# One layer of a hybrid decoder on one core: another order of the two plain feature groups, tile norms on VectorE, the keys' short product in another bank, and the last tiles worked in halves

## The chip, the cores and the metric

The kernel runs on one core of a Trainium2 chip. Time is device time of one execution, in microseconds (us); smaller is better. Six names of queues and engines return throughout: PE (TensorE, the matrix multiplications and transposes), PEld (its weight loads), DVE (VectorE), ACT (ScalarE), POOL (GpSimd) and SP (SyncE, which here only issues transfers). Each engine works through its own instructions in a fixed order and waits, at the head of that order, for what its next instruction needs.

## The reference

One layer is computed for 1024 prompt tokens with 16 meta tokens ahead of them, and for 64 sample tokens: 1104 tokens of width 1024, all in fp32.

```python
def rms_norm(x, g):  # cut
    return x * rsqrt(mean(x * x, -1) + eps) * g
def half_ffn(h, g_pre, g_post, w_gate, w_up, w_down):
    return h + 0.5 * rms_norm(swiglu(rms_norm(h, g_pre), w_gate, w_up, w_down), g_post)
# run_layer
h = half_ffn(h, ffn1_...)
y, st = token_mixer(rms_norm(h, mix_norm_pre), ...)   # u @ w_in, gated DeltaNet, sliding-window attention, @ w_out
h = h + rms_norm(y, mix_norm_post)
h = half_ffn(h, ffn2_...)
```

The hidden width of either FFN is 2816. In the DeltaNet branch each head's keys are convolved, normalised and multiplied with themselves (`kk = k k^T`, per chunk), decayed and solved against.

## The kernel before

**Precision and tiles.** Every large product is made of fp32r operands that are split into a high and a low part (`xh`, `xl`, `wh`, `wl`), with three matmuls for one. ACT rounds to the high part, DVE or POOL subtracts to get the low part. Tokens come in nine tiles of 128 rows, the last of them short, and go into the FFNs as two halves of tokens.

**Gate and up.** The 22 groups of 128 hidden features are worked in 11 pairs, `f` = 0 to 10. One pair takes, for gate and for up, seven block products instead of eight (Strassen's scheme in Winograd's form): the products `p` = 1 to 7 land in the PSUM banks A, B and C, and DVE adds them into `u2g`, `sg`, `u3g` and the like (`gate_up`, L322). `hidden(f)` (L364) then makes gate times up (on POOL, `times`) and writes to DRAM the operands that the down product reads: seven of them, with the sums `S1` and `S2`, for most pairs, but only four and no sums for the two pairs in `plain`, which are 9 and 10. Each operand is a tile `hs` (four buffers), made of a high part and a DVE subtraction, and stored to `hid`. The work of `hidden(f)` is issued step by step among the products of the pair after it. The first two pairs start while the tokens are still being transposed (`start`, L446): of these `up` (L458) then makes only the products 6, 5, 7, 4 and 3.

**Down.** `down` (L500) loads `hb` tiles from `hid` on SP's queue and `raw` weights on the same queue, and adds the products into `acc`. Pairs 9 and 10 are the last group, with plain products.

**Tails.** After the first FFN each tile of tokens is transposed back (L582), normed, added to the residual (`post_norm`, L618), normed again for the mixer (`pre_norm`, L94) and transposed again (L105). A norm is a square-and-sum on ACT (L81), two tiny POOL operations (L82, L83) for the factor, and a multiplication. In `pre_norm` the multiplication by the gain is POOL's (L99), that by the factor ACT's (L101). After the second FFN, tiles 0 to 5 are finished among the last down products, and tiles 6, 8 and 7 behind them; only tile 7 is normed in halves (`last_norm`, L625).

**Mixer.** `before` (L809) projects the beta/decay columns and the first two heads' keys while the tails run. `w_in` (L766) loads a weight column, rounds it on ACT (L773) and subtracts on POOL (L774). `gates` (L819) turns beta and decays into factors. For each head `keys` (L962) transposes the convolved keys into PSUM tiles tagged `tr`, and multiplies keys by keys into tiles `pk` (two buffers): two of 128-row blocks (L1008), and one 80x80 product of the 80 tokens that are left over (L1014). DVE reads each `pk` (L1010, L1015). `decays` (L951) adds masks on POOL (L954). Then a triangular solve runs lane by lane on DVE (`lane_solve`, L1058) beside the sliding-window attention (`swa_kv` L1104, `swa_block` L1201).

**What sets the order.** PE's order is the program's own: generators are merged by `weave` with written shares. On the other engines a scheduler of the compiler orders the instructions, except where the code pins one (`keep_in_program_order`) or holds it behind another (`issue_after`).

**The start.** The gain of the first norm comes as one row of 4 KB on ACT's queue, and PE spreads it over 128 partitions by two matmuls (L1907); DVE copies it to SBUF (L1908).

## Time and profile before

| | |
|---|---|
| median of 3 runs | 2791.03 us (2784.93 to 2792.57) |
| the profiled execution | 2782.66 us, its span 2780.8 us |
| mean granted TensorE clock | 0.982 |
| PE busy | 2663.7 us (96% of the span) |
| DVE, ACT, POOL busy | 1586.3, 1096.9, 1389.3 us |

The span runs from the first to the last instruction that the profiler saw; 1.9 us of the execution lie outside it. The profiled execution is 0.3% faster than the median of the three runs. A gap of an engine is the idle time just before an instruction, put down to what ended it last. Times of places below are us from the start of the span.

### The profile page before, as it was taken

What the parts mean: (1) busy time and instruction counts of PE and PEld (TensorE: products, weight loads), DVE (VectorE), ACT (ScalarE), POOL (GpSimd) and SP (SyncE); (2) the same over time, 40 slices, a digit from 0 to 9 for tenths busy, and PEclk for the clock granted to TensorE, in tenths of its full rate; (3) what the DMA queues carried; (4) which work ended last, traced back from release to release, by engine and by line L of the source; (5) the groups of instructions that cost most, each with busy time, mean ns of one, the idle gap of its engine ahead of it and who ended that gap; (6) DMA issues with size and microseconds to landing.
All of it is one profiled execution on the core that took longest, in us unless ns stands there. A gap on an engine that the chain in (4) does not pass through costs nothing. (4 is left out here: it accounts for less than half of the span.)

```text
span 2780.8 us, 49379 instructions
## 1 busy us (share of the span) xinstructions
PE 2663.7 (96%) x18961; PEld 2495.5 (90%) x18961; DVE 1586.3 (57%) x2381; ACT 1096.9 (39%) x2584; POOL 1389.3 (50%) x1297
## 2 busy tenths in 40 slices
PE   7999999999978998999999999998999999999998
PEld 6999999999977887788788888887789999999998
DVE  6666565345556759964544444443557566553566
ACT  5343343322154642354444444444443343334221
POOL 5555555445455744654434434435455555554472
PEclk9999999999988999999999999999999999999999
DMA  4343343577533652354323333334443343427763
GB/s 139 134 156 134 141 161 120 200 232 241 180 130 114 200 186 92 101 175 116 107 84 93 90 96 95 92 90 133 138 138 137 138 159 132 145 112 296 241 232 139
DMA packets 229412, 405.96 MB, mean 146 GB/s; under 512 B 59719, under 2 KB 121319, under 8 KB 228888
## 3 DMA queue, kind: packets, MB, share of 16 engines
q1 hardware_dynamic: 208870, 324.23, 36.0%
q10 hardware_dynamic: 20306, 78.57, 7.1%
q8 instruction: 150, 2.46, 0.4%
q14 instruction: 86, 0.70, 0.1%
HBM read 263.84 MB, written 140.53 MB: 145 GB/s over the span
## 5 line engine op out<-in xcount | busy, mean ns | idle before, releaser
L281 POOL TENSOR_TENSOR wl<-T,wh 128x512 fp32r<-128x512 f32 x246 | 330.5, 1349 | 345.1 <-ACT wh L280 254.4
L133 PE MATMUL gu<-xh,wl 128*128 128x512 f32 (+3 forms) x1456 | 500.5, 344 | 0.1
L129 PE MATMUL gu<-xh,wh 128*128 128x512 f32 (+3 forms) x1456 | 496.6, 341 | 0.0
L131 PE MATMUL gu<-xl,wh 128*128 128x512 f32 (+3 forms) x1456 | 496.0, 341 | 0.0
L495 PE MATMUL y<-hb,wh 128*128 128x256 f32 (+2 forms) x2528 | 432.2, 291 | 8.5 <-DMA hb<-hid 7.3
L281 POOL TENSOR_TENSOR wl<-raw,wh 128x512 fp32r<-128x512 f32 x200 | 281.5, 1414 | 248.8 <-ACT wh L280 198.8
L495 PEld LDWEIGHTS y<-hb,wh 128*128 128x128 f32 x2528 | 367.6, 189 | 10.4 <-DMA hb<-hid 7.9
L133 PEld LDWEIGHTS gu<-xh,wl 128*128 128x128 f32 x1456 | 280.7, 193 | 28.4 <-issue 11.1
L280 ACT CAST wh<-T 128x512 fp32r<-128x512 f32 x246 | 152.4, 620 | 377.5 <-PE B L315 117.0
L131 PEld LDWEIGHTS gu<-xl,wh 128*128 128x128 f32 x1456 | 280.5, 193 | 19.6 <-issue 1.2
L129 PEld LDWEIGHTS gu<-xh,wh 128*128 128x128 f32 x1456 | 280.5, 193 | 18.4 <-issue 1.6
L495 PE MATMUL y<-hb,wl 128*128 128x256 f32 (+2 forms) x1264 | 272.4, 289 | 0.0
L280 ACT CAST wh<-raw 128x512 fp32r<-128x512 f32 x200 | 122.2, 620 | 286.4 <-PE C L315 87.8
L506 DVE TENSOR_TENSOR acc<-acc,y 128x552 f32<-128x552 f32 (+4 forms) x216 | 145.1, 679 | 149.2 <-PE y L495 148.7
L774 POOL TENSOR_TENSOR wl<-raw,wh 128x1024 fp32r<-128x1024 f32 x60 | 144.7, 2412 | 145.5 <-ACT wh L773 126.1
L495 PEld LDWEIGHTS y<-hb,wl 128*128 128x128 f32 x1264 | 208.0, 189 | 0.0
L255 DVE TENSOR_TENSOR T<-raw,raw 128x512 f32<-128x512 f32 x124 | 120.9, 979 | 120.8 <-POOL wl L281 120.3
L1536 POOL TENSOR_TENSOR f<-f,mhalf 128x1 f32<-128x1 f32 (+1 forms) x72 | 54.4, 756 | 112.0 <-DVE f L1534 106.5
L266 DVE TENSOR_TENSOR T<-raw,T 128x512 f32<-128x512 f32 x62 | 64.4, 1042 | 59.5 <-POOL wl L281 59.5
L927 DVE SCALAR_TENSOR_TENSOR cv<-pc,cw,cv 128x1131 f32<-128x1131 f32 x48 | 75.2, 1568 | 34.2 <-POOL cv L924 33.8
L255 DVE TENSOR_TENSOR T<-raw,T 128x512 f32<-128x512 f32 x62 | 66.7, 1082 | 32.6 <-POOL wl L281 32.4
L1067 DVE TENSOR_TENSOR la<-la,ltmp 72x14 f32<-72x14 f32 (+37 forms) x76 | 80.1, 1054 | 1.3
(589 smaller groups left out, 7408.5 us busy)
## 6 DMA issues: line engine op xcount, KB each, us to landing
hb<-hid SPq DMA_DIRECT2D x71, 552.0 KB
hb<-hid SPq DMA_DIRECT2D x71, 544.0 KB
hid<-hs ACTq DMA_DIRECT2D x69, 552.0 KB
hid<-hs ACTq DMA_DIRECT2D x69, 544.0 KB
raw<-in_w_in_dram SPq DMA_DIRECT2D x58, 512.0 KB
raw<-in_ffn_w_gate_dram SPq DMA_DIRECT2D x100, 256.0 KB
raw<-in_ffn_w_up_dram SPq DMA_DIRECT2D x94, 256.0 KB
raw<-in_ffn_w_down_dram SPq DMA_DIRECT2D x88, 256.0 KB
```

Source lines behind the costliest of these rows:

```text
L129: nc.tensor.matmul(ps, wh, xh, start=first and i == 0, stop=False)
L131: nc.tensor.matmul(ps, wh, xl, start=False, stop=False)
L133: nc.tensor.matmul(ps, wl, xh, start=False, stop=last and i == n - 1)
L255: self.nc.vector.tensor_tensor(out=b[name], in0=b[x], in1=b[y], op=ALU.subtract)
L266: nc.vector.tensor_tensor(out=s, in0=b["21"], in1=s, op=ALU.subtract)
L280: self.nc.scalar.copy(hi, s)
L281: self.nc.gpsimd.tensor_tensor(out=lo, in0=s, in1=f32(hi), op=ALU.subtract)
L495: self.nc.tensor.matmul(self.view(ps[d], (i,)), w[x][:, d * P:(d + 1) * P], hb[:, y, lo:hi], start=j + x + y == 0, stop=j == len(items) - ...
L506: dve = lambda out, x, y: nc.vector.tensor_tensor(out=out, in0=x, in1=y, op=ALU.add)
L774: nc.gpsimd.tensor_tensor(out=lo, in0=raw, in1=f32(hi), op=ALU.subtract)
L927: nc.vector.scalar_tensor_tensor(out=cv, in0=pc[:, w:w + PADW], scalar=self.cw[:, j, w:w + 1], in1=cv, op0=ALU.mult, op1=ALU.add)
L1067: nc.vector.tensor_tensor(out=a[:n, 0:j, j + 1:size], in0=a[:n, 0:j, j + 1:size], in1=t, op=ALU.add)
```

## The change

Nine things are edited.

1. The pairs of either FFN are worked in the order 9, 0, 1, ..., 8, 10 (`self.order`): one plain pair first, the other last. For the last pair, gate times up is on DVE for two of the three products. A hold on the second pair's steps (`issue_after(self.sixth)`) is taken out.
2. The gain of the first norm is loaded as a broadcast of 512 KB on SP's queue, behind the first two tiles and ahead of the first weights. The row, the two matmuls and the two copies go.
3. In `sixth_ahead` the three loads are pinned; in `down` the weight difference `T1` of the first group is pinned.
4. `pre_norm` multiplies by gain and factor in one DVE instruction (L100 of the changed kernel) instead of one on POOL and one on ACT.
5. The rounding and subtraction of head 1's weights (column 9) is held behind the norm of the tile that comes before.
6. `gates` yields once more and is woven in three steps from 0.5 on instead of two from 0.75; the exponential of `ea` is pinned.
7. The keys' 80x80 product goes into the `tr` tile of the last transposes, which has three buffers now; `pk` serves the 128-row blocks alone. The masks of head 1 and later are pinned.
8. The third group of transposes of the sliding window's keys and values goes into a tile `po` instead of `pt`.
9. After the second FFN, tiles 0 to 3, and 4 and 5, are finished earlier; tiles 6, 8 and 7 are finished in halves of 512 features, the first halves among the last down products, and the second halves of 6 and 8 use PSUM tiles of the down products (`y`).

```diff
+        self.order = (plain[0], *(f for f in range(NF // 2) if f not in plain), plain[1])
...
-    nc.gpsimd.tensor_tensor(out=out[:n], in0=x[:n], in1=g[:n], op=ALU.mult)
     r = rstd(c, pool, x, n, 1.0 / D, EPS, "n")
-    nc.scalar.activation(out[:n], out[:n], AF.Copy, scale=r[:n, 0:1])
+    nc.vector.scalar_tensor_tensor(out=out[:n], in0=x[:n], scalar=r[:n, 0:1], in1=g[:n], op0=ALU.mult, op1=ALU.mult)
...
             if len(parts) == 2 and p != 6:
-
-                with self.c.tc.issue_after(self.sixth) if p in (7, 4) and (f, kind) == self.begun else nullcontext():
-                    next(self.late, None)
+                next(self.late, None)
...
         def times(key):
-            nc.gpsimd.tensor_tensor(out=g[key], in0=g[key], in1=u[key], op=ALU.mult)
+            (nc.vector if f == self.order[-1] and key != "u3" else nc.gpsimd).tensor_tensor(out=g[key], in0=g[key], in1=u[key], op=ALU.mult)
...
-                        self.difference(x, "T1", "12", "11")
+                        self.difference(x, "T1", "12", "11", c.tc.keep_in_program_order if vi == 0 else lambda op: op)
...
-        self.ready = {8 + h: self.w_in(8 + h, self.nc.scalar) for h in range(2)}
+        raw = [self.w_load(8 + h, self.nc.scalar) for h in range(2)]
+        self.ready = {8: self.w_in(8, raw[0])}
+        tc = self.c.tc
+        with tc.issue_after(self.c.last_square), tc.issue_after(self.c.last_factor):
+            self.ready[9] = self.w_in(9, raw[1])
...
                 nc.tensor.transpose(pt[:80, 0, :], k8, self.k(C_IDENT))
+                nc.tensor.matmul(pt[:80, 1, 0:80], k8, k8, start=True, stop=True)
...
-                nc.tensor.matmul(pk[:80, 0, 0:80], k8, k8, start=True, stop=True)
-                nc.vector.scalar_tensor_tensor(out=b8, in0=pk[:80, 0, 0:80], scalar=ns[:80, 8:9], in1=dt[:80, 8, 0:80],
+                nc.vector.scalar_tensor_tensor(out=b8, in0=pt[:80, 1, 0:80], scalar=ns[:80, 8:9], in1=dt[:80, 8, 0:80],
...
-                before = [(gates, 0.75, 1, 2)]
+                before = [(gates, 0.5, 1, 3)]
...
-                    pt = self.ps([P, 4, P], "pt", 2)
+                    pt = self.ps([P, 4, P], "pt", 2) if t0 < 8 else self.ps([P, 4, P], "po")
...
-                if t == 0:
-                    row, one = c.t(xin, [1, D], tag="row", bufs=1), c.t(xin, [1, P], tag="one", bufs=1)
-                    nc.scalar.dma_start(row, I["ffn1_norm_pre"])
...
+                if t == 1:
+                    gain("ffn1_norm_pre", xin)
...
+        def last_tiles(pool):
+
+            g, state = gain("ffn2_norm_post", pool), {}
+            for h, t in ((h, t) for h in range(2) for t in (6, 8, 7)):
+                n, cols = f2.rows[t], slice(512 * h, 512 * h + 512)
+                if (h, t) in ((1, 6), (1, 8)):
+                    ps = c.t(f2.psy[0], [P, 1024], tag="y").rearrange("p (k t) -> p k t", t=P)[:, 0:4]
+                else:
+                    ps = c.t(ptr, [P, KD, P], tag="tr")[:, 0:4]
+                f2.feature_half(ps, t, h)
...
+                nc.scalar.activation(dump[:n, cols], src[:n], AF.Square, accum_out=r2[:n, h:h + 1])
+                nc.vector.tensor_tensor(out=y[:n, cols], in0=src[:n], in1=g[:n, cols], op=ALU.mult)
...
-        weave((dn, 0, 1, 15), (f2.tail_steps(ptr, nrm, finish2, (0, 1, 2, None, 3, None, 4, 5)), 0.05, 0.95, 8))
-        drain(f2.tail_steps(ptr, nrm, finish2, (6, 8, 7)))
+        last = last_tiles(nrm)
+        weave((dn, 0, 1, 15), (f2.tail_steps(ptr, nrm, finish2, (0, 1, 2, 3)), 0, 0.46, 4),
+              (f2.tail_steps(ptr, nrm, finish2, (4, 5)), 0.5, 0.7, 2), (steps_of(last, 3), 0.68, 1, 3))
+        drain(last)
```

What this does to the order of instructions is shown at three places. A row is the source line, the operation, and out<-in with buffer numbers; lines behind the edits are numbered a few lower or higher in the changed kernel.

The first place is DVE in the first FFN, up to the sum `u3g` of the second pair's gate, which PE's bank C waits for. `S`, `hs` and the product with `g_` belong to `hidden` of the first pair. Before:

```order
L266 TENSOR_TENSOR T_1340<-raw_1336,T_1340 128x512
L353 TENSOR_TENSOR u2g_1184<-sg_561,B_1159 128x552
L372 TENSOR_TENSOR hs_1255<-S_198_1137,hs_1255 128x552
L372 TENSOR_TENSOR sg_241<-g_80_312,sg_241 128x552
L255 TENSOR_TENSOR T_1559<-raw_1517,raw_1515 128x512
L372 TENSOR_TENSOR hs_1292<-sg_241,hs_1292 128x552
L353 TENSOR_TENSOR sg_561<-u2g_1184,B_1226 128x552
L372 TENSOR_TENSOR hs_1326<-S_197_1136,hs_1326 128x552
L372 TENSOR_TENSOR hs_1437<-g_134_678,hs_1437 128x552
L358 TENSOR_TENSOR u3g_1252<-sg_561,C_1190 128x552
```

The same place in the changed kernel:

```order
L369 TENSOR_TENSOR hs_1127<-sg_232,hs_1127 128x552
L369 TENSOR_TENSOR hs_1203<-u2g_818,hs_1203 128x552
L369 TENSOR_TENSOR hs_1410<-g_130_669,hs_1410 128x552
L267 TENSOR_TENSOR T_1314<-raw_1310,T_1314 128x512
L354 TENSOR_TENSOR u2g_1171<-sg_552,B_1146 128x552
L256 TENSOR_TENSOR T_1532<-raw_1490,raw_1488 128x512
L354 TENSOR_TENSOR sg_552<-u2g_1171,B_1212 128x552
L357 TENSOR_TENSOR u3g_1238<-sg_552,C_1177 128x552
```

Between `u2g` and `u3g` stand two instructions now, where seven stood; the sums `S` of the first pair are gone.

The second place is POOL among the tails of the first FFN. `rp` is the factor of `post_norm`, `rn` that of `pre_norm`, `wl` the low part of a `w_in` weight column. Before:

```order
L774 TENSOR_TENSOR wl_8974<-raw_8971,wh_8973 128x1024
L774 TENSOR_TENSOR wl_8980<-raw_8977,wh_8979 128x1024
L82 TENSOR_SCALAR rp_8892<-rp_8892 128x1
L83 TENSOR_TENSOR rp_8892<-rp_8892,mhalf_64 128x1
L99 TENSOR_TENSOR res_8890<-acc_863_5982,g_mix_norm_pre_8245 128x1024
L82 TENSOR_SCALAR rn_8901<-rn_8901 128x1
L82 TENSOR_SCALAR rp_9042<-rp_9042 128x1
L83 TENSOR_TENSOR rn_8901<-rn_8901,mhalf_64 128x1
L83 TENSOR_TENSOR rp_9042<-rp_9042,mhalf_64 128x1
L99 TENSOR_TENSOR acc_864_5983<-y_9041,g_mix_norm_pre_8245 128x1024
```

In the changed kernel:

```order
L764 TENSOR_TENSOR wl_8963<-raw_8958,wh_8962 128x1024
L82 TENSOR_SCALAR rp_8880<-rp_8880 128x1
L83 TENSOR_TENSOR rp_8880<-rp_8880,mhalf_64 128x1
L82 TENSOR_SCALAR rn_8888<-rn_8888 128x1
L83 TENSOR_TENSOR rn_8888<-rn_8888,mhalf_64 128x1
L764 TENSOR_TENSOR wl_8967<-raw_8960,wh_8966 128x1024
L82 TENSOR_SCALAR rp_9029<-rp_9029 128x1
L83 TENSOR_TENSOR rp_9029<-rp_9029,mhalf_64 128x1
L82 TENSOR_SCALAR rn_9037<-rn_9037 128x1
L83 TENSOR_TENSOR rn_9037<-rn_9037,mhalf_64 128x1
```

The gain's multiplications are out of POOL's order, and the second weight column stands behind the tile's two factors.

The third place is SP's queue where the first down product begins. `hid` is written from the last pair's `hs`, `hb` reads operands of earlier pairs. Before:

```order
L248 DMA raw_6503<-in_ffn_w_down_dram 128x512
L248 DMA raw_6505<-in_ffn_w_down_dram 128x512
L390 DMA hid_6_70<-hs_5927 128x1104
L390 DMA hid_6_70<-hs_5931 128x1104
L480 DMA hb_6150<-hid_6_70 128x1104
L480 DMA hb_6225<-hid_6_70 128x1104
```

In the changed kernel:

```order
L387 DMA hid_6_70<-hs_5918 128x1104
L387 DMA hid_6_70<-hs_5922 128x1104
L249 DMA raw_6490<-in_ffn_w_down_dram 128x512
L249 DMA raw_6492<-in_ffn_w_down_dram 128x512
L249 DMA raw_6494<-in_ffn_w_down_dram 128x512
L477 DMA hb_6141<-hid_6_70 128x1104
L477 DMA hb_6216<-hid_6_70 128x1104
```

The two stores of the last pair stand ahead of four weight loads (6490 to 6496, which were 6499 to 6505) that stood ahead of them; three of these are between them and the first `hb` load, the fourth behind it.

More of the change, by code (lines that the diff above doesn't have):

```diff
@@ L1 @@
 import itertools
-from contextlib import ExitStack, nullcontext
+from contextlib import ExitStack
 import numpy as np
@@ L80, in rstd @@
         dump = c.t(pool, [P, D], BF16, tag="dump", bufs=1)
-    pin(nc.scalar.activation(dump[:n], x[:n], AF.Square, accum_out=r[:n]))
+    c.last_square = pin(nc.scalar.activation(dump[:n], x[:n], AF.Square, accum_out=r[:n])).ins
     nc.gpsimd.tensor_scalar(out=r[:n], in0=r[:n], scalar1=scale, scalar2=eps, op0=ALU.mult, op1=ALU.add)
-    nc.gpsimd.tensor_tensor(out=r[:n], in0=r[:n], in1=c.mhalf[:n, 0:1], op=ALU.pow)
+    c.last_factor = nc.gpsimd.tensor_tensor(out=r[:n], in0=r[:n], in1=c.mhalf[:n, 0:1], op=ALU.pow).ins
     return r
@@ L193, in __init__ @@
         self.X = {p: [None, None] for p in range(1, 8)}
-        self.st, self.ready, self.early, self.fin, self.late, self.begun = {}, {}, {}, {}, iter(()), None
+        self.st, self.ready, self.early, self.fin, self.late = {}, {}, {}, {}, iter(())
     def x_tiles(self, pool, p, parts):
@@ L236, in right, with raw @@
             yield
-    def raw(self, kind, fs, names):
+    def raw(self, kind, fs, names, pin=lambda op: op):
         b = [{} for _ in fs]
@@ L291, in ahead @@
                 b = {name: r[:, 512 * (p - 1):512 * p]}
-                self.ready[0, kind, p] = self.w_op(b, p)
+                self.ready[self.order[0], kind, p] = self.w_op(b, p)
     def sixth_ahead(self):
-        b, = self.raw("g", (0,), ("11", "12", "22"))
+        b, = self.raw("g", self.order[:1], ("11", "12", "22"), self.c.tc.keep_in_program_order)
         t = self.c.t(self.rawp, [P, 512], tag="raw")
@@ L299, in sixth_ahead @@
             self.nc.vector.tensor_tensor(out=out, in0=x, in1=y, op=ALU.subtract)
-        self.ready[0, "g", 6] = self.w_split(self.wp, b["22"])
+        self.ready[self.order[0], "g", 6] = self.w_split(self.wp, b["22"])
     def view(self, ps, parts):
@@ L380, in split @@
             hs = c.t(self.hsp, [P, 2, self.half], F32R, tag="hs")
-            if f == NF // 2 - 1 and p not in (1, 4):
+            if f == self.order[-1] and p not in (1, 4):
                 nc.vector.tensor_copy(hs[:, 0], s)
@@ L386, in split, with store @@
             stores.append((self.h_d[f, p - 1].rearrange("p (x t) -> p x t", x=2), f32(hs)))
-        def store(queue=nc.sync if f == NF // 2 - 1 else nc.scalar):
+        def store(queue=nc.sync if f == self.order[-1] else nc.scalar):
             for x in stores:
@@ L444, in open_rest, with start @@
         self.hsp = self.c.pool(es, "hs", bufs=4, side=side)
-    def start(self, f, split):
+    def start(self, i, split):
+        f = self.order[i]
         b = self.early.pop(f, None) or {k: {} if (f, k, 1) in self.ready else self.raw(k, (f,), ("11", "21"))[0]
@@ L458, in up @@
     def up(self, started):
-        self.begun = started - 1, "g"
-        for f in range(NF // 2):
+        for i, f in enumerate(self.order):
             for kind in "gu":
                 b, = self.raw(kind, (f,), ("11", "12", "22", "21"))
-                for p in (6, 5, 7, 4, 3) if f < started else (1, 6, 5, 7, 2, 4, 3):
+                for p in (6, 5, 7, 4, 3) if i < started else (1, 6, 5, 7, 2, 4, 3):
                     drain(self.gate_up(f, kind, (p,), b))
@@ L568, in down, with feature_half @@
                     yield from block(q, column, second, ds, (i,))
-    def end(self, psum, pool, t, finish):
+    def feature_half(self, ps, t, h):
         c, nc, a = self.c, self.nc, self.acc
@@ L574, in end @@
         tl = a[6][:, :, 0:4 * self.tail].rearrange("p i (j t) -> p i j t", j=2)
-        for q, i, o in {4: ((2, 0, 0), (3, 2, 0)), 8: ((4, 0, self.tail), (5, 2, self.tail))}.get(t, ()):
-            nc.scalar.copy(tl[:, i:i + 2, :, o:o + self.tail],
-                           a[q][:, :, 512:].rearrange("p (i j) t -> p i j t", j=2))
+        if t in (4, 8):
+            q, o = (2, 0) if t == 4 else (4, self.tail)
+            nc.scalar.copy(tl[:, 2 * h:2 * h + 2, :, o:o + self.tail],
+                           a[q + h][:, :, 512:].rearrange("p (i j) t -> p i j t", j=2))
+        for d in range(4):
+            src = tl[:, 2 * h + d // 2, d % 2] if t == 8 else a[(2 if t < 4 else 4) + h][:, d, t % 4 * P:t % 4 * P + P]
+            nc.tensor.transpose(ps[:n, d, :], src, c.ident)
+    def end(self, psum, pool, t, finish):
+        c, n = self.c, self.rows[t]
         ps = c.t(psum, [P, KD, P], tag="tr")
-        for d in range(KD):
-            q = ((2, 3) if t < 4 else (4, 5))[d // 4]
-            src = tl[:, d // 2, d % 2] if t == 8 else a[q][:, d % 4, t % 4 * P:t % 4 * P + P]
-            nc.tensor.transpose(ps[:n, d, :], src, c.ident)
+        for h in range(2):
+            self.feature_half(ps[:, 4 * h:4 * h + 4], t, h)
         self.fin[t] = finish(t, n, ps.rearrange("p k t -> p (k t)"), pool, psum)
@@ L953, in decays @@
         nc, dt = self.nc, self.x[h]["dt"]
-        nc.gpsimd.tensor_tensor(out=dt[:, 0:8, :], in0=dt[:, 0:8, :],
-                                in1=self.k(C_MNEG).unsqueeze(1).to_broadcast([P, 8, P]), op=ALU.add)
+        pin = self.c.tc.keep_in_program_order if h else lambda op: op
+        pin(nc.gpsimd.tensor_tensor(out=dt[:, 0:8, :], in0=dt[:, 0:8, :],
+                                    in1=self.k(C_MNEG).unsqueeze(1).to_broadcast([P, 8, P]), op=ALU.add))
         nc.gpsimd.tensor_tensor(out=dt[:80, 8, :80], in0=dt[:80, 8, :80], in1=self.k(C_MNEG8, 80, 80), op=ALU.add)
@@ L972, in keys @@
         for t0 in (0, 4, 8):
[L973 removed]
+            pt = self.ps([P, 4, P], "tr", 3)
             if t0 < 8:
@@ L1914, in tiles_in @@
             load(1)
-            f1.early[0] = {kind: f1.raw(kind, (0,), ("11", "21"))[0] for kind in "gu"}
+            f1.early[f1.order[0]] = {kind: f1.raw(kind, f1.order[:1], ("11", "21"))[0] for kind in "gu"}
             for t in order[2:7]:
```

87 lines of the change are left out of this document (42 added, 45 removed).

## The prediction

> **What bounds the kernel now.** I read the busy times first, then PE's waits, then the granted clock behind them, and last the single places. The page's first part:
>
> ```profile
> PE 2663.7 (96%) x18961; PEld 2495.5 (90%) x18961; DVE 1586.3 (57%) x2381; ACT 1096.9 (39%) x2584; POOL 1389.3 (50%) x1297
> ```
>
> PE is idle for only 2780.8 - 2663.7 = 117 us, and the change leaves its matmuls as they are but for two at the start. So what it can give lies in these 117 us and in what they drag behind them. The view of PE's waits (engine, line, what ended the wait: us in total, times, longest) names them:
>
> ```profile
> PE C L315 <- DVE u3g L358: 10.9, 4, 4.2
> PE tr L105 <- ACT res L101: 9.8, 2, 5.8
> PE pk L1014 <- DVE bm L1010: 8.6, 4, 4.5
> PE y L495 <- DMA hb<-hid: 7.3, 5, 4.3
> PE tr L105 <- ACT acc L101: 5.0, 2, 2.7
> PE tr L1907 <- DMA row<-in_ffn_norm_pre_dram: 4.8, 1, 4.8
> PE pt L1136 <- DVE vtl L1140: 4.2, 1, 4.2
> PE tr L877 <- ACT gc L875: 3.8, 1, 3.8
> PE tr L207 <- POOL x L229: 2.5, 2, 1.7
> ```
>
> The change touches what each of these waits for. A long wait costs a second time: behind it PE runs at half clock. By windows of time (window and length; busy us of PE, PEld, DVE, ACT, POOL; granted clock, DMA share, GB/s):
>
> ```profile
> 116.90:123.70 6.80, 4.60 (x20) 4.63 (x21) 3.98 (x5) 1.85 (x3) 2.11 (x2) 0.50 0.63 243
> 540.10:546.90 6.80, 5.52 (x24) 5.53 (x25) 0.00 (x0) 1.24 (x2) 0.00 (x0) 0.50 1.00 384
> 792.70:799.50 6.80, 5.26 (x25) 5.26 (x26) 1.75 (x2) 3.81 (x6) 3.94 (x5) 0.50 0.44 154
> 809.80:813.20 3.40, 3.40 (x18) 3.40 (x17) 1.28 (x1) 1.52 (x4) 1.95 (x1) 0.50 0.38 141
> 830.30:837.10 6.80, 5.12 (x26) 5.09 (x27) 0.49 (x1) 2.04 (x4) 0.00 (x0) 0.50 0.20 58
> 864.40:871.20 6.80, 5.11 (x17) 4.86 (x18) 1.95 (x5) 3.47 (x11) 0.78 (x5) 0.50 0.45 150
> 888.30:895.10 6.80, 5.62 (x18) 4.83 (x19) 3.61 (x11) 6.57 (x23) 2.11 (x5) 0.50 0.66 252
> 1055.50:1058.90 3.40, 3.26 (x12) 3.26 (x13) 3.33 (x5) 0.00 (x0) 0.00 (x0) 0.51 0.00 0
> 2123.90:2127.30 3.40, 3.40 (x16) 3.40 (x17) 1.26 (x2) 1.10 (x2) 0.89 (x1) 0.50 0.50 204
> ```
>
> Half of PE's busy time in each is lost: 2.3, 2.8, 2.6, 1.7, 2.6, 2.6, 2.8, 1.6 and 1.7 us. A term below is a wait and the lost half behind it.
>
> **The second pair (a plain pair comes first).** Of the waits for `u3g` the two long ones end at 119.10 and 2123.79, one in each FFN. They sum to 8.3 us (10.9 less two short ones of 2.6 together). Ahead of the second one stand, in the chain of waits and on DVE:
>
> ```profile
> 2116.93 4.29 DMA hid<-hs
> 2121.25 1.17 DVE L372 TENSOR_TENSOR hs<-g,hs 128x544 fp32r<-128x544 f32 x1
> 2122.94 0.71 DVE L358 TENSOR_TENSOR u3g<-sg,C 128x544 f32<-128x544 f32 x1
> ```
>
> DVE is behind because it first finishes the seven operands of pair 0, for the last of which it needs an `hs` buffer that a store gives back. With pair 9 first there are four operands for four buffers, and no sums; two DVE instructions stand between `u2g` and `u3g` instead of seven. Both waits should go: 8.3 + 2.3 + 1.7 = 12.3; I take 12. The seven operands of pair 0 now fall to the third pair, which has all fourteen products as cover, as every later pair had without a long wait for `u3g`. Bounds: 9 (a gap of 1.5 us stays in each) and 12.3.
>
> **Start of down.** The wait for `hb` that ends at 541.38 is 4.3 us.
>
> ```profile
> 527.91 1.59 POOL L376 TENSOR_TENSOR u2g<-u2g,u2u 128x552 f32<-128x552 f32 x1
> 534.13 1.45 SPq L390 DMA_DIRECT2D hid<-hs  x2
> 535.68 0.99 SPq L480 DMA_DIRECT2D hb<-hid  x2
> ```
>
> SP's queue reaches the two stores at 534, and the `hb` loads behind them; DMA is full (1.00 in the window). With the product on DVE (about 0.7 us, as `u3g`'s row, instead of 1.59) and the stores ahead of four weight loads, I estimate that the stores' 1.1 MB move ahead by some 4 us, and `hb` with them: product and queue's arrival lie 534.1 - 529.5 = 4.6 us apart now. The three loads between cost 0.75 MB / 384 GB/s = 2 us of the gain. Term: 4.3 + 2.8 = 7.1 at best, 0 if those loads still wait for their buffers; 5 taken.
>
> **Tile norms.** The four waits on L101 sum to 14.8 us. The rows on POOL, DVE, ACT and PE:
>
> ```profile
> 782.67 4.73 POOL L774 TENSOR_TENSOR wl<-raw,wh 128x1024 fp32r<-128x1024 f32 x2 [1.04 <-ACT wh L773]
> 788.23 1.29 DVE L622 SCALAR_TENSOR_TENSOR acc<-acc,rp,res 128x1024 f32<-128x1024 f32 x1 [0.25 <-POOL rp L83]
> 809.60 0.97 PE L105 MATMUL tr<-ident,acc 128*128 128x128 f32 x4 [2.26 <-ACT acc L101]
> 825.73 2.39 POOL L99 TENSOR_TENSOR res<-y,g_mix_norm_pre 80x1024 f32<-80x1024 f32 x1 [1.86 <-DVE y L622]
> 829.38 1.28 ACT L840 ACT_TABLE_LOAD   x1
> 830.79 1.13 ACT L101 ACTIVATE res<-res,rn 80x1024 f32<-80x1024 f32 x1
> ```
>
> Now the multiplication (2.39) runs on POOL ahead of the factor, and ACT's 1.13 behind it: 3.5 us beside the factor's two small operations, which stay. After: ACT's square, about 1.1 (L101's shape), ahead of the factor, and one DVE multiplication of about 1.29 (L622's row has the same form) behind it: 2.4 us, so 1.1 less on each of four waits. The first tile also loses one of the two L774 (2.4 us) ahead of its factor, and the last loses the table load with its exponential (1.5), which the pin puts later, but no more than its wait allows: 2.6. That makes 3.5, 1.1, 1.1 and 2.6, together 8.3 of 14.8. Of the half clocks 809.80 and 830.30 should go (4.3), 792.70 may stay with a rest of 2.2 us. 12.6 in sum; I take 11, since DVE has the tails' other work in the same order. Bounds 5 and 14.8 + 6.9 = 21.7.
>
> That the 2.26 us wait alone is followed by a half clock is this row and the 809.80 window. The Trainium skill (TensorE: Matmul & The Clock Gate, "What's actually happening") puts the half clock behind a whole idle window of about 3.4 us; by it this wait costs no clock, and the sum would be an estimated 1.7 us less. The trace disagrees (0.50 in the row), and I go by the row.
>
> **Gates.** The wait for `gc` ends at 866.09:
>
> ```profile
> 864.71 1.15 ACT L930 ACTIVATE th<-cv 128x1131 f32<-128x1131 f32 x1 [3.96 <-DVE cv L927]
> ```
>
> The 72-column copy stands behind this activation, which waits for DVE. Woven earlier, the copy comes ahead of it, twelve matmuls before PE needs it. 3.8 + 2.6 = 6.4 at best, 3 if DVE's factors come late after the later exponential; 5 taken.
>
> **Keys.** The longest wait for a `pk` tile ends at 889.48. On POOL and DVE:
>
> ```profile
> 878.94 2.38 POOL L954 TENSOR_TENSOR dt<-dt,cst 128x1024 f32<-128x1024 f32 x1
> 878.61 6.56 DVE L927 SCALAR_TENSOR_TENSOR cv<-pc,cw,cv 128x1131 f32<-128x1131 f32 x1
> 885.21 1.39 DVE L927 SCALAR_TENSOR_TENSOR cv<-pc,cw,cv 128x1131 f32<-128x1131 f32 x1
> ```
>
> The third use of two `pk` buffers waits for DVE's reads of the first, and DVE is late because one L927 took 6.56 us beside three masks in a row, where the next took 1.39. The short product needs no `pk` now, and the masks are spread. All four waits and the half clock would be 8.6 + 2.8 = 11.4; 9 taken, lower bound 6 (the late DVE shows on another tile).
>
> **Window keys.** The wait for `vtl`, 4.2 + 1.6 = 5.8, goes, since the third transposes need no `pt`. But in the stretch it stands in, DVE is full:
>
> ```profile
> 1028.00:1195.00 167.00, 152.60 (x898) 134.17 (x898) 163.07 (x244) 54.21 (x151) 89.44 (x77) 0.96 0.32 100
> ```
>
> 163 of 167 us: the solve and the attention share DVE in an order that stays, so PE gets there earlier and waits later. 0 taken; bounds 0 and 5.8.
>
> **Start.**
>
> ```profile
> 5.00:10.00 5.00, 3.54 (x4) 0.93 (x4) 1.91 (x3) 3.15 (x7) 2.78 (x6) 1.00 0.99 341
> 9.48 3.50 DVE L90 SCALAR_TENSOR_TENSOR x<-x,rn,g 128x1024 f32<-128x1024 f32 x2 [0.21 <-DVE g L1908]
> ```
>
> The row's wait of 4.8 is no gain by itself: PE has nothing else yet. The gain tile is ready at 9.3 now; as 512 KB behind two tiles of 512 KB, at 341 GB/s from about 2 us, it lands near 7, but all weights behind it come 512 KB / 341 GB/s = 1.5 us later. That nets 0 (from 2 us gained to 2 lost). Pinned loads let the token sums run earlier: of the waits for L229 (2.5 shown, some 2.4 more in smaller rows) I take 3. Bounds: 2 lost, 6 gained.
>
> **Last tiles.**
>
> ```profile
> 2764.66 0.93 PE L582 MATMUL tr<-ident,acc 128*128 128x128 f32 x7
> 2776.23 1.41 DVE L638 SCALAR_TENSOR_TENSOR y<-y,rp,acc 128x512 f32<-128x512 f32 x2 [0.95 <-POOL rp L636]
> ```
>
> Now 24 transposes and three norms follow the last product, 13 us to the last multiplication's end. After, 12 transposes move ahead (1.2 us at 0.1 each), and behind the last product stand seven short DVE steps and three wide ones: I get an end near 2775.6 instead of 2777.6. 2 taken, bounds 0 and 4.
>
> **The sum.** 12 + 5 + 11 + 5 + 9 + 0 + 3 + 2 = 47 us off the profiled 2782.66, that is 2735.7. That execution was 8.4 us faster than the median of the runs, so I set the forecast against the median: 2791 - 47 = 2744. The lower bounds sum to 9 + 0 + 5 + 3 + 6 + 0 - 2 + 0 = 21 (2770), the upper to 75 (2716).
>
> **Rivals.**
>
> *Given back before the solve.* Keys, gates and window keys (14 us) are only moved: the DVE-full stretch sets the pace. For it: the 163 of 167. Against it: the solve's input comes from the keys, so its start moves ahead with them. Time 2791 - 33 = 2758.
>
> *The stall moves to the third pair.* Pair 0's seven operands and the new first waits meet there: 12 us come back, 2791 - 35 = 2756. For it: the four `hs` buffers stay four. Against it: later pairs showed no such wait.
>
> *All of it goes.* Every wait and its half clock vanish: upper bounds of all but the window keys and half the tiles, 75 - 6 - 8 = 61, so 2730.
>
> *Slower: VectorE and GpSimd block each other in the solve.* The 6.56 against 1.39 us shows 5.2 us lost for one DVE instruction. In 1028 to 1195 DVE has no room and POOL has 77 instructions; should the shifted streams meet there, each such meeting is on the path. It decides from (47 + 8) / 5.2 = 11 meetings; 12 give 2744 + 62 = 2806. Against it: both orders stay as they are in that stretch, and the meetings it has today are in the time already. The Trainium skill (SBUF — State Buffer, "SBUF: two separate sides") states that the port pair of VectorE and GpSimd is an exclusive lock, also against a VectorE instruction with two SBUF inputs. The new L100 is such an instruction, so by that page the one L774 that stays among the tiles could hold one of them for an estimated 2.4 us, and the sum would be 45. The trace agrees that they block (6.56); whether they meet here, no row shows.
>
> **How the numbers follow.** Forecast 0.6, given back 0.15, third pair 0.1, all 0.1, slower 0.05. The range, 2717 to 2772, reaches from the upper bounds' sum to just past the lower's; the slower rival and a mix of the two that give back are left out. About 0.3% (8 us) is what a measurement of this kernel can tell from no change. Faster by more: 0.87, from all cases but the slower one and some of the two that give back; same 0.07; slower 0.06.
>
> **What would show it.** No wait over 2 us for `u3g` in either FFN; none for `pk` or for the tile that now holds the short product; the waits on DVE's `pre_norm` under 7 us in sum; none over 2 us for `hb` at 530 to 545 or for `gc`; full clock at 117, 541, 864, 888 and 2124; new waits between 1090 and 1195 that grow by about 5 us. I am wrong if PE's idle time falls by less than 25 us, or if the waits fall and the clock does not follow.

## The result

The changed kernel takes 2743.47 us (median of 4 runs, 2738.05 to 2747.16), the kernel before 2790.72 us in the same set: a ratio of 0.9833, 95% interval 0.9811 to 0.9855. That is 47 us less (41 to 53). In a second set, as `after_again` below, it took 2739.2 us. The page's first part after the change:

```profile
span 2741.2 us, 49395 instructions
PE 2654.0 (97%) x18957; PEld 2491.2 (91%) x18957; DVE 1587.4 (58%) x2396; ACT 1086.3 (40%) x2579; POOL 1359.7 (50%) x1283
```

The profiled span is 39.6 us shorter, less than the medians say, since the profiled execution of the kernel before was 8 us faster than its median. PE's idle time fell from 117.1 to 87.2 us, by 29.9; PE's busy time fell by 9.7, of which 3.75 are the two matmuls at the start. PE's waits after the change, in the view shown before:

```profile
PE tr L208 <- DVE x L90: 10.4, 2, 8.9
PE sc L1216 <- DVE s L1219: 4.2, 2, 3.7
PE y L492 <- DMA hb<-hid: 3.9, 3, 1.8
PE C L316 <- DVE u3g L357: 3.1, 2, 1.9
PE tr L104 <- DVE res L100: 2.9, 1, 2.9
PE tr L872 <- ACT gc L870: 2.8, 1, 2.8
```

The long waits for `u3g`, `bm` and `vtl` are gone and `hb` has halved; `gc` has only fallen from 3.8 to 2.8, and a new wait for `s` stands at 1040. The first line is the start itself, where PE has no other work. The longer of the two waits for `u3g` that are left is not at the second pair but at the first, where the kernel before waited 1.4 us:

```profile
79.05 0.36 PE L316 MATMUL C<-x30h,wh 128*128 128x256 f32 x1 [1.92 <-DVE u3g L357]
```

I set PE's instructions of both traces side by side, matched by their operands and their count, and read at each place how far the changed kernel is ahead (its lead). The steps add up to 39.7 us:

| place (us of before) | lead gained | forecast |
|---|---|---|
| start, to 100 | 4.4 | 3 |
| second pair, first and second FFN | 7.3 + 6.7 | 12 |
| start of down, 541 | 5.8 | 5 |
| end of down, 675 to 770 (not edited) | -2.0 | - |
| tile norms, 770 to 840 | 5.9 | 11 |
| gates, 840 to 875 | 3.1 | 5 |
| keys, 875 to 1000 | 13.1 | 9 |
| window keys, 1050, and the solve up to 1080 | 5.9 - 5.7 | 0 |
| solve to second FFN, 1080 to 2060 (not edited) | -6.9 | - |
| second down, to 2750 (not edited) | -0.5 | - |
| last tiles | 2.6 | 2 |

The edited places gave 49.1 us against 47 forecast. Places that nobody edited lost 9.4 in this execution.

### The profile page after: what moved, and what is told of

The parts are those of the page before. It is cut to its first block, busy times and chain, and to the rows that moved or that the text cites. A ratio compares the mean times of both kernels' runs of the same rounds, so it can differ in the third digit from the quotient of the medians.

```text
span 2741.2 us, 49395 instructions
## 1 busy us (share of the span) xinstructions
PE 2654.0 (97%) x18957; PEld 2491.2 (91%) x18957; DVE 1587.4 (58%) x2396; ACT 1086.3 (40%) x2579; POOL 1359.7 (50%) x1283
## 5 line engine op out<-in xcount | busy, mean ns | idle before, releaser
L922 DVE SCALAR_TENSOR_TENSOR cv<-pc,cw,cv 128x1131 f32<-128x1131 f32 x48 | 66.9, 1396 | 27.0 <-POOL cv L919 26.7
L1061 DVE TENSOR_TENSOR ltmp<-la 72x14 f32<-72x14 f32 (+37 forms) x76 | 70.8, 932 | 12.4 <-DMA la<-b_d 11.1
```

The lines of the kernel that those rows point to most:

```text
L922: nc.vector.scalar_tensor_tensor(out=cv, in0=pc[:, w:w + PADW], scalar=self.cw[:, j, w:w + 1], in1=cv, op0=ALU.mult, op1=ALU.add)
L1061: nc.vector.tensor_tensor(out=t, in0=a[:n, 0:j, j:j + 1].to_broadcast([n, j, w]), in1=a[:n, j:j + 1, j + 1:size].to_broadcast([n, j, w]), ...
```

## The experiments

All of them start from the changed kernel unless said otherwise, and undo or alter one piece. The executions were made in several sets. The median of the changed kernel itself moved by 4 us from one set to another, so the verdicts rest on the traces at the place, and the median only says whether the total agrees. A loss at a place holds the half clocks next to it, and these differ between executions too.

### The same kernel again

> The changed kernel unchanged, a second time. In the first trace the lead over the kernel before shrinks by 4.9 us between 1960 and 2060 and by 2.7 us between 1325 and 1385, places that the change does not edit. Theory A (these are half-clock windows that fall differently, since several waits there are just under or over 2 us): a second execution keeps the same waits within 0.3 us each, but its half-clock windows in those stretches sit elsewhere, and the lead there differs by 2 to 5 us from the first trace; the whole time stays within 2738 to 2748. Theory B (the change does it, through another alignment of engines): the same waits and the same windows, the lead shrinks again by 4 to 5 and 2 to 3 us at those places.

The median is 2739.2 us (2736.7 to 2741.02). Nearly all waits above 1 us come back within 0.4 us. The exceptions are small at 79 (`u3g`, 1.9 and 2.5) and larger in the second FFN: the transposes at 1965 (2.2 and none) and at 2011 (1.6 and 2.4), and the first matmul on `x11h` behind them (2.6 and 1.0). The half clocks do move. The windows view gives the busy time of PE, its weight loads, DVE, ACT and POOL in a stretch, with the number of instructions, and then the granted clock. Here are the 20 us around those waits, first of the kernel before:

```profile
2043.00:2063.00 20.00, 16.09 (x110) 14.55 (x111) 9.33 (x18) 8.98 (x19) 13.46 (x11) 0.91 0.19 60
```

The changed kernel there, in its first execution:

```profile
2009.00:2029.00 20.00, 15.66 (x86) 13.62 (x86) 9.30 (x16) 8.18 (x18) 11.62 (x10) 0.74 0.13 46
```

And in its second:

```profile
2009.00:2029.00 20.00, 16.29 (x110) 14.88 (x111) 10.62 (x19) 8.96 (x20) 14.55 (x11) 0.91 0.17 57
```

The waits in it add up to 4.1, 4.2 and 3.7 us; yet the clock is 0.91, 0.74 and 0.91, and between the two executions of the changed kernel that is 24 matmuls in the same 20 us. The second execution is 3.3 us ahead of the first in this stretch, so most of the 4.9 us lost there is where the half clocks fell: theory A. At 1343 both executions of the changed kernel have a half clock, as theory B says. PE's timeline, in the first of them:

```profile
1338.27 0.67 PE L1452 MATMUL tr<-R,xt 64*64 64x64 f32 x8 [0.79 <-ACT vs L1448]
1341.78 1.16 PE L1463 MATMUL tr<-qv,kf 128*128 128x128 f32 x8 [1.42 <-ACT sqp L1477]
1344.16 0.48 PE L1504 MATMUL tr<-kq 128*64 128x64 f32 x2 [0.78 <-DVE pm L1465]
```

Its clock behind them:

```profile
1344.00:1348.00 4.00, 3.84 (x14) 3.26 (x15) 0.86 (x3) 1.63 (x3) 1.10 (x1) 0.59 0.21 45
```

The kernel before had the same three waits, and the clock stayed full:

```profile
1380.00:1384.00 4.00, 3.22 (x22) 2.82 (x22) 1.49 (x5) 1.64 (x3) 1.07 (x1) 1.00 0.14 30
```

Two executions are not enough for theory B, though. Of the kernels below, `b1_nohold`, which is the kernel before with a single edit in the FFNs, has 3.4 us of half clock behind these waits (at 1383.9), and `e2_prenorm` and `e5_row`, which keep nearly all of the change, have none behind the same three waits (clock 1.00 from 1342 on and from 1343.5 on). That the change causes the half clock here is not shown.

### The order of the pairs, and the hold

```diff
-        self.order = (plain[0], *(f for f in range(NF // 2) if f not in plain), plain[1])
+        self.order = tuple(range(NF // 2))
```

> The changed kernel with only the order of the pairs put back to 0, 1, ..., 10 (so pair 0 with seven operands is first again, 9 and 10 last); the hold behind the sixth product stays out. Between the two traces the lead grew by 7.3 us at the second pair of the first FFN and by 6.7 us in the second. Theory A (the seven operands of the first pair make VectorE late): both waits for u3g come back, each about 4 us with a half clock behind it, and the time grows by 12 to 15 us. Theory B (the hold that was taken out, or the other order of VectorE behind it, did it): the waits stay under 2 us and the time grows by less than 4 us.

The median is 2744.57 us, 5 more than `after_again`'s 2739.2 in another set. The wait that comes back at the second pair is another one, for `u2g`. In the first FFN (window 75 to 125; 2.5 of the 2.8 us for `u3g` are the first pair's, as in `after_again`):

```profile
PE C L316 <- DVE u3g L357: 2.8, 2, 2.5
PE B L316 <- DVE u2g L354: 2.2, 1, 2.2
```

At the place 3.0 us are lost in the first FFN and 3.9 in the second, where a wait of 2.0 us for `u2g` is followed by a half clock of 3.4 us at 2088. Together that is 6.9 us, not 12 to 15. Theory A is out as the whole cause, and theory B's limit of 4 us is passed too. So the hold that the change takes out was tried on the kernel before, alone:

```diff
-                with self.c.tc.issue_after(self.sixth) if p in (7, 4) and (f, kind) == self.begun else nullcontext():
-                    next(self.late, None)
+                next(self.late, None)
```

> The kernel before with one edit of the change alone: the hold of the second pair's steps behind the sixth product is taken out; the order of the pairs stays 0 to 10. The changed kernel with the old order and no hold kept waits of 2.2 and 2.1 us only (for u2g, not u3g) and lost 5 us, not the 12 to 15 that the order alone should have been worth. Theory A (the hold was the larger half of the cause): the two waits for u3g of 4.2 and 4.1 us fall to about 2 us each and move to u2g, a half clock stays behind one of them at most, 6 to 9 us less than the kernel before. Theory B (the waits belong to the seven operands and came back smaller only because other parts of the change gave VectorE room): the waits for u3g stay at 3.5 us or more and the time falls by less than 3 us.

The median is 2782.5 us against 2788.01, a ratio of 0.9981 (0.997 to 0.9992). The same window, in the first FFN:

```profile
PE B L315 <- DVE u2g L353: 2.1, 1, 2.1
PE C L315 <- DVE u3g L358: 1.4, 1, 1.4
```

The 4.2 us wait for `u3g` has become 2.1 us for `u2g`; the 1.4 us are the first pair's. At the places 3.4 and 2.6 us are gained, 6.0 together. The waits move as theory A says, but the hold is not the larger half: it is some 6 of the 14 us, the order some 7. The two were measured on different kernels, one on the kernel before and one on the changed kernel, so that they simply add up is not shown.

### The start of down

```diff
-            (nc.vector if f == self.order[-1] and key != "u3" else nc.gpsimd).tensor_tensor(...)
+            nc.gpsimd.tensor_tensor(...)
...
-                        self.difference(x, "T1", "12", "11", c.tc.keep_in_program_order if vi == 0 else lambda op: op)
+                        self.difference(x, "T1", "12", "11")
```

> The changed kernel with only the start of down put back: the last pair's products on GpSimd for all three keys, and the weight difference T1 not pinned; the order of the pairs stays. Between the traces the lead grew by 5.8 us here. Theory A (the products' place and the pin move the stores): the wait for hb at 527 grows from 1.3 to about 4 us with a half clock behind it, 4 to 7 us more. Theory B (the plain pair at the end alone, with its four operands and the freer queue, brings it): the wait stays under 2 us, less than 1.5 us more at 550.

The median is 2741.32 us. PE's wait in the window 515 to 545, of this kernel:

```profile
PE y L492 <- DMA hb<-hid: 4.4, 1, 4.4
```

It was 1.6 in the changed kernel; a half clock of 6.8 us follows, and 5.1 us are lost at the place. Theory A. The products' place and the pin were put back together, so how much each gives is open. In the total only 2 us show (2739.2 in the other set), which is how much the rest can hide.

### The tile norms and the weight columns

The norm alone put back:

```diff
+    nc.gpsimd.tensor_tensor(out=out[:n], in0=x[:n], in1=g[:n], op=ALU.mult)
     r = rstd(c, pool, x, n, 1.0 / D, EPS, "n")
-    nc.vector.scalar_tensor_tensor(out=out[:n], in0=x[:n], scalar=r[:n, 0:1], in1=g[:n], op0=ALU.mult, op1=ALU.mult)
+    nc.scalar.activation(out[:n], out[:n], AF.Copy, scale=r[:n, 0:1])
```

> The changed kernel with only the tile norm put back: gain on GpSimd, factor on ScalarE. Theory A (as predicted, one wait per tile grows by what the norm costs): the waits before the second transposes at 770 to 815 grow from 8.7 us (2.9 + 1.8 + 1.5 + 2.1 and small ones) by 1.1 us each on four waits, 4 to 6 us in all, and the time by 4 to 8 us against the changed kernel. Theory B (the norm's place is indifferent, what helped was the other order of the weight columns' work): under 2 us more. Theory C (the multiplication on VectorE delays the tile's other steps so much that it costs): the waits shrink and the kernel is faster than the changed one.

The median is 2736.63 us, 2.6 less than `after_again` in the same set, with overlapping intervals (0.9796 to 0.9827 against 0.9803 to 0.9835). PE's waits from 765 to 820, first with the norm on VectorE (`after_again`):

```profile
PE tr L104 <- DVE res L100: 2.8, 1, 2.8
PE tr L104 <- issue: 2.1, 1, 2.1
PE tr L104 <- DVE acc L625: 1.8, 1, 1.8
PE tr L579 <- DVE acc L625: 1.7, 1, 1.7
PE tr L104 <- DVE y L625: 1.7, 2, 1.2
PE gu L132 <- POOL wl L764: 0.2, 1, 0.2
```

Put back:

```profile
PE tr L105 <- ACT res L101: 6.5, 2, 3.6
PE tr L105 <- ACT acc L101: 3.2, 3, 1.8
PE tr L580 <- DVE acc L626: 1.5, 1, 1.5
```

The waits sum to 10.3 us with the norm on VectorE and to 11.2 without: 0.9 us, not the 4 to 6 of theory A. By PE's position from 772 to 850, 1.0 us is lost against the first execution and 2.4 against the second, with the half clocks between. Two waits are 0.8 and 0.7 us longer, the others shorter. With the norm on VectorE four of the waits are for L625, which reads a transpose tile and so frees it, and one for the norm itself. VectorE's order shows why (first execution of the changed kernel; PE's wait of 1.8 us ends at 793.09):

```profile
790.62 1.28 DVE L100 SCALAR_TENSOR_TENSOR acc<-y,rn,g_mix_norm_pre 128x1024 f32<-128x1024 f32 x1
791.82 1.22 DVE L625 TENSOR_TENSOR acc<-tr,g_ffn_norm_post 128x1024 f32<-128x1024 f32 x1
```

The new multiplication stands ahead of L625 in one order, and delays it. For the norm this is theory B. Then the hold on weight column 9 alone was taken out:

```diff
-        self.ready = {8: self.w_in(8, raw[0])}
-        with tc.issue_after(self.c.last_square), tc.issue_after(self.c.last_factor):
-            self.ready[9] = self.w_in(9, raw[1])
+        self.ready = {8 + h: self.w_in(8 + h, raw[h]) for h in range(2)}
```

> The changed kernel with only the hold on weight column 9 taken out, so both columns' low parts may stand ahead of tile 3's factor on GpSimd, as before. Putting the norm itself back cost nothing. Theory A (the columns' order is what helped among the tiles): the wait at 776 grows from 2.9 to 4.5 to 5.5 us, the waits of the stretch by 2 us in sum, the time by 2 to 4 us. Theory B (nothing among the tiles hangs on it): the waits stay within 0.5 us of 9.2 us in sum.

The median is 2739.05 us. GpSimd works both columns ahead of the factor again, as its timeline shows:

```profile
766.24 4.74 POOL L764 TENSOR_TENSOR wl<-raw,wh 128x1024 fp32r<-128x1024 f32 x2 [0.86 <-ACT wh L763]
770.95 0.18 POOL L82 TENSOR_SCALAR rp<-rp 128x1 f32<-128x1 f32 x1
```

PE's wait for it, from the waits of the same kernel:

```profile
PE tr L104 <- DVE res L100: 4.6, 1, 4.6
```

The wait grows by 1.8 us and the waits of the stretch from 10.3 to 12.6 in sum, as theory A says, so the hold is worth more than the norm's new place. The time is another matter: PE falls back by 0.6 us at the place against the first execution and by 2.0 against the second, and the median stays. That the time follows is not shown.

### The gates

In the changed kernel `gc` starts late (ScalarE):

```profile
842.91 0.29 ACT L870 COPY gc<-tr 128x72 f32<-128x72 f32 x1 [2.60 <-DVE ngc L866]
```

```diff
-        nc.vector.tensor_scalar(out=self.ngc, in0=v9(pg[:, 0, :]), ...)
-        yield
-
         gc = c.t(tp, [P, 72], tag="gc")
         nc.scalar.copy(gc.rearrange("p (h t) -> p t h", h=H), v9(pg[:, 0, :]))
+        nc.vector.tensor_scalar(out=self.ngc, in0=v9(pg[:, 0, :]), ...)
+        yield
```

> The changed kernel with two program lines swapped in the gates: the copy gc on ScalarE stands ahead of the negation ngc on VectorE; both read the same PSUM tile. In the changed kernel PE still waits 2.84 us for gc, which began only when ngc, behind six wide VectorE instructions, had been done. Theory A (the copy waits for ngc because both read one tile): gc starts about 2.6 us earlier, right behind the activation at 840, the wait falls from 2.84 to under 0.5 us, and the half-clock window near 844 or later goes with it or not: 2 to 5 us less. Theory B (the copy waits for ScalarE's own queue or for PE): the wait stays at 2.5 to 3 us, no change in time.

The median is 2733.25 us, 6 less than `after_again` beside it (ratios 0.9796, 0.9779 to 0.9814, and 0.9819, 0.9803 to 0.9835: the intervals overlap). ScalarE's timeline:

```profile
839.56 0.27 ACT L867 COPY gc<-tr 128x72 f32<-128x72 f32 x1
...
842.51 0.26 ACT L880 ACTIVATE e<-ngc 128x72 f32<-128x72 f32 x1 [2.47 <-DVE ngc L868]
```

PE's, of the same kernel:

```profile
878.99 0.31 PE L975 MATMUL tr<-ident,k 128*80 128x128 f32 x1 [1.50 <-DVE b L1011]
```

Theory A: two reads of one PSUM tile by two engines ran in program order, and the copy had waited for VectorE's queue. The Trainium skill (PSUM — Partial Sum Buffer, "PSUM bank collisions raise a hardware error") says that the compiler makes two engines' accesses to one bank and quadrant depend on each other, reads against reads too; the 2.60 us that went away with the order agree. The wait is gone, 2.9 us at the place; 40 us later PE waits 1.5 us for a `tr` tile that now holds the short product until VectorE has read it, and 1.7 us are given back. 1.2 us stay, by the trace.

The same, with the subtractions of weight columns 8 and 9 on VectorE:

```diff
-        nc.gpsimd.tensor_tensor(out=lo, in0=raw, in1=f32(hi), op=ALU.subtract)
+        (low or nc.gpsimd).tensor_tensor(out=lo, in0=raw, in1=f32(hi), op=ALU.subtract)
...
-            self.ready[9] = self.w_in(9, raw[1])
+            self.ready[9] = self.w_in(9, raw[1], self.nc.vector)
```

> The swap of gc and ngc, and in addition the low parts of the first two weight columns (8 and 9) subtracted on VectorE instead of GpSimd, so that GpSimd's in-order queue among the tile norms holds only the factors. In the changed kernel one of these subtractions took 3.45 us and stood ahead of a tile's factor, and PE waited 2.86 us for the norm at 775.8 and 0.92 us for the low part at 777.9. Theory A (GpSimd's queue sets these two waits): the factor of tile 3 comes 1.2 us earlier, the waits there fall from 3.8 to about 1.5 us, and the half clock at 777.3 (6.8 us long, 2.5 to 3 us lost) goes: 4 to 6 us beside the 2 to 5 of the swap, 6 to 11 us under the changed kernel. Theory B (VectorE's order is the limit there): the subtractions, 1.3 us each, push the norms by as much, 0 to 1 us in that stretch.

The median is 2734.21 us, 1 us over the swap alone. The waits from 765 to 820 are 9.4 us in sum, near the 10.2 of the first execution, the longest 3.8 for `xl` on VectorE. By the waits this is theory B: taking work from GpSimd's order puts it into VectorE's. By PE's position the kernel gains 4.1 us on the swap alone between 772 and 850, as theory A has it, but there it has 6.8 us of half clock and the swap alone has 17. Whether the edit did that or the half clocks only fell otherwise, no run shows.

And the swap together with the norm put back, the edits of `i1_gc` and `e2_prenorm` in one kernel:

> The changed kernel with the swap of gc and ngc and with the tile norm put back to GpSimd and ScalarE, the two edits that were measured one by one at 6.0 and 2.6 us under the changed kernel in the same set of runs. By the traces the swap takes away the wait of 2.9 us at 842 and gives 1.5 us back at a later wait for a tr tile at 878. Theory A (the medians say what the edits do): 2729 to 2733 us. Theory B (only what is seen at the place counts, 1 to 2 us, and the rest was half-clock windows that fell well): 2734 to 2739 us.

The median is 2735.0 us, inside theory B's range and above A's: the two gains of 6.0 and 2.6 do not add. None of these three kernels is clear of the changed kernel.

### The keys' short product

```diff
-                nc.tensor.matmul(pt[:80, 1, 0:80], k8, k8, start=True, stop=True)
...
+                nc.tensor.matmul(pk[:80, 0, 0:80], k8, k8, start=True, stop=True)
```

> The changed kernel with only the keys' 80x80 product put back into a third pk tile of two buffers; the masks stay pinned and the tr tiles stay three. Between 866 and 1000 the lead grew by 14 us from one trace to the other. Theory A (a third use of two buffers makes PE wait for VectorE's reads): waits for pk come back, 5 to 9 us in sum over the heads, with one half-clock window of 2 to 3 us: 6 to 11 us more. Theory B (the three masks in a row that slowed VectorE were the cause; spread masks leave it in time): the waits for pk stay under 3 us in sum, and the time grows by less than 3 us.

The median is 2746.08 us. PE's waits from 830 to 1000:

```profile
PE pk L1010 <- DVE bm L1006: 4.3, 3, 2.7
PE tr L872 <- ACT gc L870: 3.0, 1, 3.0
```

4.3 us of the former 8.6 return, with a half clock at 878; 6.6 us are lost between 850 and 970, and the total is 6.9 over `after_again` in another set. That is theory A at its lower end; the waits are just under its 5 us. The other half of the 13 us is not in the product. In the changed kernel the three L922 at 870 to 874 take 1.39 to 1.40 us each beside no mask, where the kernel before had one of 6.56 us beside three; that the pinned masks gave this half was not tried alone. Some of the loss has moved: VectorE's next wide multiplication, L991, takes 2.95 us at 875.56 where it took 1.35 before, but no wait of PE follows it.

### The window's keys

```diff
-                    pt = self.ps([P, 4, P], "pt", 2) if t0 < 8 else self.ps([P, 4, P], "po")
+                    pt = self.ps([P, 4, P], "pt", 2)
```

> The changed kernel with only the third group of window transposes back in a pt tile. In the first trace the lead grew by 5.9 us at 1050 and fell by 5.1 us 25 us later, where PE waits 3.73 us for s on VectorE. Theory A (given back: VectorE is full there and sets the pace): the wait of about 4.2 us for vtl returns, the wait of 3.7 us for s shrinks to under 1.5 us, the time stays within 1.5 us by the trace at 1100. Theory B (the gain is real and the later wait has another cause): the wait for s stays at 3.7 us and the time grows by 4 to 6 us.

The median is 2738.67 us. PE's waits from 1005 to 1100, changed kernel first:

```profile
PE sc L1216 <- DVE s L1219: 4.2, 2, 3.7
PE pt L1233 <- POOL m L1226: 2.6, 2, 1.8
```

Then with the old place:

```profile
PE pt L1132 <- DVE vtl L1136: 3.6, 1, 3.6
...
PE sc L1216 <- DVE s L1219: 1.0, 2, 0.8
```

The wait is the same one at another instruction: PE is 6.2 us behind at 1020 and level again at 1040. Theory A.

### The first gain

```diff
-                if t == 1:
-                    gain("ffn1_norm_pre", xin)
+                if t == 0:
+                    ...  # row, two matmuls and two copies, as before
```

> The changed kernel with only the first norm's gain put back to a row of 4 KB that PE spreads; the pinned loads stay. Between the traces the lead was 1.9 us at the first transposes, and 7.3 us at 60. Theory A (the broadcast load gains the 1.9 us of the start, the pinned loads the rest): first transposes 1.5 to 2.5 us later, the waits for the token sums at 45 to 60 stay small, 2 us more in all. Theory B (the 512 KB delay the weights by as much as the gain is early): the first matmuls of the weights come at the same time or earlier, and nothing is lost or even 1 us gained. Theory C (the change at the start does all of the 7 us): 5 us or more are lost.

The median is 2735.14 us, not more than the others. At the place it loses 3.0 us (first transposes at 11.93 instead of 8.92), which are still lost at 80. That is more than theory A's 2 us and less than theory C's 5. The total does not show it: by 810 the lead is back, and from 1290 to 1980 six more are gained where the half clocks fell otherwise.

## Why the prediction was right, and where it was not

The median came out at 2743.47 where 2744 was forecast. The mechanism, waits of PE that go and a clock that recovers behind them, held at most places; that the number is so close is partly luck, since errors of the steps in both directions cancelled.

**What bounds the kernel** held: PE's idle time gave 29.9 us, three quarters of the profiled gain. Of the signs that were named, full clock came at all five places, and the long waits for `u3g`, `pk` and `hb` went. The wait for `gc` stayed over 2 us, and the new wait on VectorE stands at 1040, which is about 1080 of the kernel before and ahead of the 1090 that was named.

**The second pair** was right in size (14.0 against 12, above its bound of 12.3) and half wrong in its cause. The prediction put all of it on four operands instead of seven; the hold that the change also takes out was named in the edit and not priced. Alone it is worth 6.0 us, and the order, put back alone, 6.9.

**Start of down**: 5.8 against 5. Putting back the products' place and the pin together loses 5.1 of it, so the mechanism named is the right one.

**Tile norms** is the step that failed. 11 us were taken and 5.9 came at the place. The step counted, per tile, 1.1 us from moving the multiplication; undone, that is worth 0.9 us of waits over all tiles. The note "DVE has the tails' other work in the same order" was right and should have been the main term: L625, L120 and L100 share VectorE, and the waits moved to them. The waits of the stretch fell from 14.8 to 10.2 us, by 4.6 where 8.3 were counted. Of the three half clocks two stayed in the first execution: matched by PE's instructions, those at 792.70 and 809.80 are these of the changed kernel, and only the one at 830.30 is gone (the second execution has 3.4 us each at 776 and 810):

```profile
777.30:784.10 6.80, 6.21 (x29) 6.21 (x30) 3.17 (x3) 1.80 (x4) 1.99 (x5) 0.50 0.70 219
794.40:797.80 3.40, 3.40 (x18) 3.40 (x17) 1.65 (x2) 2.00 (x4) 0.74 (x2) 0.50 0.44 154
```

Whether VectorE and GpSimd meet here, which the prediction left open, the changed kernel's trace answers. They do, once:

```profile
774.32 1.28 DVE L100 SCALAR_TENSOR_TENSOR res<-acc,rn,g_mix_norm_pre 128x1024 f32<-128x1024 f32 x1 [1.59 <-POOL rn L83]
774.38 3.45 POOL L764 TENSOR_TENSOR wl<-raw,wh 128x1024 fp32r<-128x1024 f32 x1
```

L100 took its usual 1.28 us, and GpSimd's subtraction, which began 0.06 us behind it, 3.45 where the one before took 2.39. The cost was 1.1 us on GpSimd's side, ahead of the next factor.

**Gates**: 3.1 against 5. The step said that the copy would come twelve matmuls ahead of its use. It was issued there but waited 2.60 us for `ngc`, its fellow reader of the PSUM tile, behind VectorE's convolutions. With the two swapped, 2.9 us come off at the place and 1.7 are given back 40 us later.

**Keys**: 13.1 against 9; the short product is about half of it. The rest is put down to the spread masks, which no run shows alone.

**Window keys**: 0 taken, 0.2 measured, for the reason given.

**Start and last tiles**: 4.4 against 3, 2.6 against 2.

**The half clocks** came out right at the edited places and wrong in the total. The terms held seven of them, 16.5 us at their best and some 14 after what was taken off each term. Six of the seven are gone in the first execution; only that of 809.80 stayed. From the mean granted clock (given to three digits, so each figure may be off by 3 us), a span of 2780.8 us at 0.982 has 100 us at half speed, 2741.2 at 0.984 has 88, and the second execution 2737.5 at 0.986 has 77: they fell by 12 to 23 us of half clock, 6 to 12 us of time. So part of what the edited places won was lost at others, which the prediction did not count. The first three of these windows of the changed kernel were at full speed in the old trace, and the last had 3.4 us there instead of 10.2:

```profile
736.30:739.70 3.40, 3.40 (x18) 3.40 (x18) 0.84 (x2) 0.00 (x0) 0.00 (x0) 0.50 0.01 6
1040.10:1046.90 6.80, 6.12 (x25) 6.12 (x26) 6.80 (x12) 1.11 (x5) 1.43 (x2) 0.50 0.32 118
1965.10:1968.50 3.40, 3.40 (x11) 2.43 (x10) 3.40 (x4) 1.56 (x3) 2.24 (x2) 0.50 0.44 134
2016.30:2026.50 10.20, 9.93 (x41) 8.58 (x41) 4.65 (x8) 3.22 (x9) 3.47 (x4) 0.50 0.14 49
```

That the total was still met has two sources: the edited places gave 2 us more than the sum, and against the median the kernel before was 8 us slower than in the profiled execution, which about offsets the 9.4 us lost elsewhere. The second is luck. Of the rivals, the given-back one came true for the window keys only. The stall at the third pair did not come: the one wait for `u3g` of 1.9 us is at the first pair. Not all of it went: 2.8 us for `gc` and 10.2 among the tiles stay. The contention in the solve did not grow: VectorE is busy for 163.07 of 167 us there in both kernels (1028 to 1195 before, 990 to 1157 after).

## What to carry to other kernels

A wait that is removed is worth its length only if the engine that caused it has room behind it: ask what that engine does next, and undo each edit alone before naming a cause, a hold or pin that goes with it included. Where the clock depends on idle time, judge an edit of a few us by its waits and by PE's position at the place, in more than one execution, and not by the total, since half clocks elsewhere move the total by as much. Before a copy is moved earlier, look for a second reader of its PSUM tile that is issued ahead of it.

## What was not expected of the hardware

The same waits are followed by a half clock in one execution and not in the next. Three waits of 0.79, 1.42 and 0.78 us, in the same order, had none behind them in the kernel before (1374 to 1381) and a half clock of 3.4 us at 1344 in the changed kernel and 6.8 us when it ran again; waits of 4.1 us in sum at the second FFN were followed by 3.4 us of half clock before, 4.2 us by 10.2 after. The Trainium skill (TensorE: Matmul & The Clock Gate, "What's actually happening") has the clock halve after an idle window of about 3.4 us and calls the window free-running. No single wait in these places is that long, so the traces do not agree with a full idle window; that the outcome changes between executions of one kernel fits a window that runs on its own. In these traces waits well under 2 us were thus enough when several fell together. Two edits with a visible loss at their place (3.0 us at the start, 5.1 us at down) moved the median by only -4 and +2 us from `after_again`, in other sets.
